# Weight remainders and branch sums made by accumulating transfers in a two-layer mixer trunk

## The chip, the core and the metric

The kernel runs on one core of a Trainium2 chip. The metric is the device time in microseconds of one execution of the whole program. The engines are TensorE (PE, matrix products), VectorE (DVE), ScalarE (ACT), GpSimd (POOL) and SyncE (SP, which only issues transfers). Each has its own instruction stream and runs it in order; transfers run on 16 shared engines of their own.

## The reference

Two layers over 512 latent tokens and 256 context tokens of width 1024, in float32. Cut to what matters here:

```python
h = rms(x) * (1 + scale) + shift             # scale, shift, gate from a small conditioning product
cols = h @ w_in                              # one projection, split for four mixers and their gates z
o_a = attention(q_a, k_a, v_a)               # rotary q and k, latent queries see all keys
o_d = windowed_attention(q_d, k_d, v_d, sink)
o_b = fourier_mix(b) ; o_c = spatial_gate(u, v)
y = stack([o * silu(z) for o, z in ...]) @ w_br          # per branch, to width 1024
g = sigmoid(h @ w_merge + b_merge)                       # per branch and channel
x = x + gate * (sum_over_branches(g * y) @ w_out)
```

In the second layer the context tokens are read but not updated.

## The kernel before

**Float32 products in three passes.** TensorE works on float32r, a rounded float32. To keep float32 accuracy every weight and every activation is held as two tiles: `hi`, the rounded value, and `lo`, the remainder (value minus `hi`). A product is then `hi*hi + hi*lo + lo*hi`, three matmuls into the same PSUM bank: L185, L186 (both with the weight's `wh`) and L188 (with the weight's `wl`).

**Weights come in pieces.** A list `plan` has 320 pieces in the order in which the program uses them: 256 of 128x512 elements (256 KB) and 64 of 128x256 (128 KB, the branch projections `w_br`). `wload` (L154) issues the load of a piece on SP into a raw tile `wr` (L159); `wround` (L162) casts it on ACT into `wh` (L169) and subtracts on POOL, or on DVE for one piece in three, into `wl` (L171). `wnext` (L174) is called when the program comes to a piece: it asks for loads up to five pieces on and for splits up to two on, so that when piece i is used, piece i+1 is being split. There are three buffers each of `wr`, `wh`, `wl`. A raw buffer is free for the next load when the subtraction has read it.

**Stages.** The start squares and norms x, computes the conditioning (`ada_tile`, weights `aw`) and, in the same loop over eight k-tiles, the first projection from pieces of its own (`wst`, tiles `ws`, split on ACT and POOL at L393 and L394). Each layer then projects (`proj`, `vproj`: `vproj("v")`, `uproj`, `qblock`, `zblock`, `bproj`), prepares rotary q and k (`Rope.finish`, with tables `cos` and `sin` loaded once into the constant tile `krope` at L405), rearranges them by transfers (`stack_k` L526, `stack_q` L513), and does attention with the projections and the merges of branches C and A as filler between its matmuls. Then come the merges of D and B (`merge`) at full matmul rate, and the output projection (`outp`). `merge` makes for each of eight channel tiles j a gate product (two pieces) and a branch product (one half piece), applies tanh on ACT (L669) and the product on DVE (L671) into a tile `g`, and adds it into `M[j]` at L674: on POOL for A and D, on DVE for the last branch B. Beside the merges and the output projection of layer 0 runs `ada_rest`, the conditioning of the second layer (64 loads `wadat` on SP, 128 reductions on DVE at L274).

**Between the layers** `outp` does its context-and-first-latent columns `c_a` and the rest `c_b` separately, and the second layer's first projection (`kv`, sixteen pieces `wkv`, first pass over 512 columns, second over 256) starts while the norms of the new x are applied (`Norm.apply`, L353 to L356).

**What sets the order.** Generators interleave the parts in program order, by estimated costs (`drive`, `paced`, `mix`); each engine's stream is then laid out from that order by the tile framework, which may move an instruction past others that it does not depend on.

Of the kernel before, what the change touches and what calls it, by code (L numbers as in the profile page):

```python
# [12 lines left out]
F32 = dt.float32  # L13
F32R = dt.float32r
BF16 = dt.bfloat16
AF = mybir.ActivationFunctionType
ALU = mybir.AluOpType
AX = mybir.AxisListType

P = 128  # L20
D = 1024
KT = 8
NL = 512
# [6 lines left out]
LOADS, W_RAW, W_HI, W_LO = 5, 3, 3, 3  # L30
# [17 lines left out]
def hybrid_trunk(tc, xt, cv, crow, win, wst, wkv, wm, wo, wada, wadat, sm, bsp, wsp, wfn, kc, krope, kmask,  # L48
                 kdft, dfl, dfc, out):
    nc = tc.nc  # L50
# [6 lines left out]
    with ExitStack() as es:  # L57
# [15 lines left out]
        def tl(tag, name, dtype=F32):  # L73
            return pools[tag].tile([P, NT], dtype, name=name, tag=tag)
# [77 lines left out]
        loaded, ready = [], []  # L152
# [9 lines left out]
        def wround(upto):  # L162

            while len(ready) < min(upto, len(plan)):
                i = len(ready)
                n, raw = plan[i][1], loaded[i]
                hi = pw.tile([P, 512], F32R, name=f"wh{i}", tag="whi", bufs=W_HI)
                lo = pw.tile([P, 512], F32R, name=f"wl{i}", tag="wlo", bufs=W_LO)
                A.copy(hi[:, :n], raw[:, :n])  # L169
                on_v = i % 3 == 0 if both[0] <= i < both[1] else i % 3 == 2 and i >= 24  # L170
                (V if on_v else G).tensor_sub(lo[:, :n], raw[:, :n], hi[:, :n].bitcast(F32))  # L171
                ready.append((hi, lo))

        def wnext():  # L174

            i = cnt[0]
            cnt[0] += 1
            wload(i + LOADS)
            wround(i + 2)
            return ready[i]  # L180
# [191 lines left out]
        rt_ = pc.tile([P, 2 * NL], F32, name="krope")  # L372
        cos, sin = rt_[:, :NL], rt_[:, NL:]
# [10 lines left out]
        for kk in range(KT):  # L384
# [9 lines left out]
            G.tensor_sub(wl[:, :512], wraws[kk][:, :512], wh[:, :512].bitcast(F32))  # L394
            if kk == 0:
                lat4 = [bank(f"st{b}", "mm" if b < 3 else "o") for b in range(4)]
                ctx4 = pps.tile([P, 1024], F32, name="stc", tag="s")
# [7 lines left out]
        nc.sync.dma_start(rt_, krope)  # L405
# [6 lines left out]
        for l in range(DEPTH):  # L412
# [9 lines left out]


# [31 lines left out]
            class Rope:  # L455
# [16 lines left out]
                def finish(self):  # L472
# [9 lines left out]
                    yield  # L482
                    r = tl("sc", f"r{name}")
# [162 lines left out]
            def merge(r, first=False, final=False, ctag="mm"):  # L646
                yb = YB[r]
                mlp = mq = None
                for j in range(KT):
# [23 lines left out]
                    if not first:  # L673
                        (V if final else G).tensor_add(M[j][:, WC], M[j][:, WC], g[:, WC])  # L674
# [228 lines left out]
            def stacks_a():  # L903

                yk = yield from rk.finish()
# [10 lines left out]
            def stacks_d():  # L916
                yq = yield from RQ[1].finish()
                yield from stack_q(Q[1], *yq, f"1{l}")
# [275 lines left out]
```

## Time and profile before

| | us |
|---|---|
| median of 3 runs | 1218.69 |
| lowest, highest | 1217.77, 1220.76 |
| the profiled execution, its own time | 1220.09 |
| its span, first to last instruction | 1218.2 |
| PE busy in the span | 1183.5 |
| DVE busy | 658.7 |
| ACT busy | 470.7 |
| POOL busy | 392.2 |

Busy time is the union of an engine's instructions; matmuls overlap, so their durations are longer than the distance from one start to the next. The profile page also gives the share of time in which the 16 transfer engines were busy, the queues' bytes, the waits of each engine by what ended them, and the chain of work that ended last.

### The profile page before, as it was taken

To read this page: it belongs to the slowest core of one execution; us is meant where nothing else is said; L and a number is where in the kernel's file an instruction comes from. 1 tells how busy PE (TensorE), PEld (TensorE's weight loads), DVE (VectorE), ACT (ScalarE), POOL (GpSimd) and SP (SyncE) were. 2 spreads that over 40 slices of the span, in tenths; PEclk is the share of its full clock that TensorE was granted. 3 is DMA by queue.
4 is the path that set the end of the run, shared out by engine and by line. 5 is a ranking of instruction groups with operands and counts; after the bars stand their busy time and mean duration, and the time that the engine had idled before them with its cause. 6 is when DMAs were issued, how large, how long until landed. Compare 5 with 4: busy or idle time off the path is not lost.

```text
span 1218.2 us, 18950 instructions
## 1 busy us (share of the span) xinstructions
PE 1183.5 (97%) x7164; PEld 1004.2 (82%) x7164; DVE 658.7 (54%) x1325; ACT 470.7 (39%) x933; POOL 392.2 (32%) x292
## 2 busy tenths in 40 slices
PE   5999999999999999999999998989999999999998
PEld 3798888888888888888888887877788888888887
DVE  5673446443455442588988667646645554232331
ACT  5334634333333332322333255445444444333431
POOL 1322333212212234454222234442222233454332
PEclk8999999999999999999999999999999999999999
DMA  7717213211111113345555653373322212333353
GB/s 282 256 31 172 79 37 83 73 36 61 53 44 49 44 56 83 93 153 160 180 165 193 183 163 110 117 194 75 99 62 69 71 56 77 101 87 100 95 166 124
DMA packets 73499, 131.99 MB, mean 108 GB/s; under 512 B 8769, under 2 KB 19137, under 8 KB 73409
## 3 DMA queue, kind: packets, MB, share of 16 engines
q1 hardware_dynamic: 66640, 120.30, 33.8%
q10 hardware_dynamic: 6768, 10.50, 2.8%
q8 instruction: 56, 0.92, 0.3%
q14 instruction: 35, 0.28, 0.1%
HBM read 115.03 MB, written 4.19 MB: 98 GB/s over the span
## 4 chain that ended last, share of the span: by engine, by line
PE 86%; DVE 5%; DMA 4%; issue 2%; ACT 2%; POOL 1%; SPq 1%; ACTq 0%; POOLq 0%
PE gl L185 10%; PE gl L186 10%; PE gl L188 10%; PE o L631 4%; PE gc L185 3%; PE tp L598 3%; PE gc L188 3%; PE gc L186 3%; PE ow L185 3%; PE ow L186 3%; PE ow L188 3%; PE yl L185 2%; PE yl L186 2%; PE yl L188 2%; PE p L185 2%; PE p L188 2%
## 5 line engine op out<-in xcount | busy, mean ns | idle before, releaser
L171 POOL TENSOR_TENSOR wl<-wr,wh 128x512 fp32r<-128x512 f32 (+1 forms) x222 | 287.5, 1297 | 703.7 <-ACT wh L169 665.4
L169 ACT CAST wh<-wr 128x512 fp32r<-128x512 f32 (+1 forms) x320 | 184.5, 577 | 354.3 <-PE gl L186 92.4
L185 PE MATMUL gl<-hh,wh 128*128 128x512 f32 x512 | 204.2, 399 | 0.0
L186 PE MATMUL gl<-hl,wh 128*128 128x512 f32 x512 | 200.2, 391 | 0.0
L188 PE MATMUL gl<-hh,wl 128*128 128x512 f32 x512 | 199.9, 391 | 0.0
L574 DVE TENSOR_REDUCE mx<-s 128x1 f32<-128x768 f32 (+3 forms) x80 | 61.6, 770 | 131.5 <-PE s L568 67.4
L171 DVE TENSOR_TENSOR wl<-wr,wh 128x512 fp32r<-128x512 f32 (+1 forms) x98 | 68.9, 703 | 116.8 <-ACT wh L169 116.5
L188 PEld LDWEIGHTS gl<-hh,wl 128*128 128x128 f32 x512 | 96.1, 188 | 21.1
L185 PEld LDWEIGHTS gl<-hh,wh 128*128 128x128 f32 x512 | 96.5, 188 | 16.6 <-issue 0.2
L186 PEld LDWEIGHTS gl<-hl,wh 128*128 128x128 f32 x512 | 96.5, 189 | 16.2
L274 DVE CUSTOM_DVE_ANT_0 aj<-at,cb 128x512 f32<-128x512 f32 x128 | 107.1, 876 | 1.5 <-DMA at<-in_wadat_dram 1.5
L582 ACT ACTIVATE p<-s,ng 128x768 f32<-128x768 f32 (+3 forms) x80 | 60.1, 751 | 97.1 <-DVE ng L579 55.5
L185 PE MATMUL gc<-hh,wh 128*128 128x256 f32 x256 | 73.5, 287 | 0.0
L188 PE MATMUL gc<-hh,wl 128*128 128x256 f32 x256 | 72.5, 283 | 0.0
L186 PE MATMUL gc<-hl,wh 128*128 128x256 f32 x256 | 72.3, 283 | 0.0
L185 PE MATMUL p<-hh,wh 128*128 128x512 f32 (+1 forms) x192 | 71.1, 370 | 0.2 <-DVE z L539 0.2
L185 PE MATMUL ow<-MH,wh 128*128 128x512 f32 (+1 forms) x200 | 69.5, 348 | 1.3 <-DVE nq1a L343 0.9
L188 PE MATMUL ow<-MH,wl 128*128 128x512 f32 (+1 forms) x200 | 69.4, 347 | 0.9 <-DVE wl L171 0.9
L186 PE MATMUL ow<-ML,wh 128*128 128x512 f32 (+1 forms) x200 | 69.4, 347 | 0.0
L188 PE MATMUL p<-hh,wl 128*128 128x512 f32 (+1 forms) x192 | 68.4, 356 | 0.0
L186 PE MATMUL p<-hl,wh 128*128 128x512 f32 (+1 forms) x192 | 68.1, 355 | 0.0
L669 ACT ACTIVATE g<-gl,bmh 128x512 f32<-128x512 f32 x64 | 43.8, 685 | 62.2 <-DVE macc L274 37.0
(466 smaller groups left out, 2583.6 us busy)
## 6 DMA issues: line engine op xcount, KB each, us to landing
wr<-in_wm_dram SPq DMA_DIRECT2D x128, 256.0 KB, 2.7
wr<-in_win_dram SPq DMA_DIRECT2D x72, 256.0 KB, 2.9
at<-in_wadat_dram SPq DMA_DIRECT2D x64, 256.0 KB, 2.8
wr<-in_wo_dram SPq DMA_DIRECT2D x40, 256.0 KB, 3.0
aw<-in_wada_dram SPq DMA_DIRECT2D x16, 512.0 KB, 5.8
wr<-in_wm_dram SPq DMA_DIRECT2D x64, 128.0 KB, 2.2
ks<-yk SPq DMA_DIRECT2D x32, 192.0 KB, 4.2
wr<-in_wkv_dram SPq DMA_DIRECT2D x16, 256.0 KB, 2.7
```

Of the source, the lines that this page charges most:

```text
L169: A.copy(hi[:, :n], raw[:, :n])
L171: (V if on_v else G).tensor_sub(lo[:, :n], raw[:, :n], hi[:, :n].bitcast(F32))
L185: T.matmul(d, wh, xh[:, c0:c1], start=first and op, stop=False)
L186: T.matmul(d, wh, xl[:, c0:c1], start=False, stop=False)
L188: T.matmul(d, wl, xh[:, c0:c1], start=False, stop=last and cl)
L274: V.tensor_tensor_reduce(out=junk[:, :512], in0=w[:, :512], in1=cb[2 * v + half][:, :512], scale=0.5, scalar=0.0, op0=ALU.mult, op1=ALU.ad ...
L574: V.reduce_max(out=mx, in_=sv, axis=AX.X)
L582: A.activation(p[:, :nk], sv, AF.Exp, bias=ng, scale=0.125, accum_out=sm_)
L598: T.transpose(tp[:, (i - g0) * P:(i - g0 + 1) * P], p[:, i * P:(i + 1) * P], ident)
L631: T.matmul(dst[64 * hx:64 * hx + 64, :], vt[kt_ // 3][:, kt_ % 3, c0:c0 + 64], pts[hx][:, j * P:(j + 1) * P], start=(j == 0), stop=(j == l ...
L669: A.activation(g[:, q0:q1], gp, AF.Tanh, scale=0.5, bias=bmh[:, r * 8 + j:r * 8 + j + 1])
```

## The change

- `wround` no longer subtracts. ACT writes `lo` as minus the raw piece, rounded as `hi` is (so `lo = -hi`), then `hi`, and POOL issues a transfer that reads the piece from DRAM again and adds it into `lo` (`accum_op=ALU.add`). All 320 pieces go this way; the raw buffer is free when ACT has read it twice.
- The buffers become 2 of `wr`, 5 each of `wh` and `wl`, and `wnext` splits up to five pieces on (piece i+4 when piece i is taken) and loads up to seven on.
- In the start's loop, at its third k-tile, the first seven loads and five splits of `plan` are asked for.
- In `merge`, the sums into `M[j]` of branches A and D become transfers from `g` to `M[j]` with the same addition, issued by POOL. Branch B stays on DVE.
- The rotary tables leave the constant tile (4 KB per partition): `tables` loads cos and sin, 256 KB each, on ACT's queue into two tiles of the pool `z`, once for the group of `stacks_a` and once for that of `stacks_d` in each layer.

```diff
-LOADS, W_RAW, W_HI, W_LO = 5, 3, 3, 3
+W_RAW, W_HI, W_LO, AHEAD = 2, 5, 5, 5
...
-                n, raw = plan[i][1], loaded[i]
+                (src, n), raw = plan[i], loaded[i]
...
+                A.activation(lo[:, :n], raw[:, :n], AF.Copy, scale=-1.0)
                 A.copy(hi[:, :n], raw[:, :n])
-                on_v = i % 3 == 0 if both[0] <= i < both[1] else i % 3 == 2 and i >= 24
-                (V if on_v else G).tensor_sub(lo[:, :n], raw[:, :n], hi[:, :n].bitcast(F32))
+                G.dma_start(lo[:, :n], src, accum_op=ALU.add)
...
-            wload(i + LOADS)
-            wround(i + 2)
+            wload(i + AHEAD + W_RAW)
+            wround(i + AHEAD)
...
+            if kk == 2:
+                wload(AHEAD + W_RAW)
+                wround(AHEAD)
...
-        nc.sync.dma_start(rt_, krope)
...
+            def tables(name):
+                if not TAB:
+                    for i in range(2):
+                        t = tl("z", f"rt{i}{name}")
+                        nc.scalar.dma_start(t[:, :NL], krope[:, i * NL:(i + 1) * NL])
+                        TAB.append(t[:, :NL])
+                return TAB
...
                     if not first:
-                        (V if final else G).tensor_add(M[j][:, WC], M[j][:, WC], g[:, WC])
+                        if final:
+                            V.tensor_add(M[j][:, WC], M[j][:, WC], g[:, WC])
+                        else:
+                            G.dma_start(M[j][:, WC], g[:, WC], accum_op=ALU.add)
```

Three places in the engines' streams. In the names, the number behind a tile's name counts pieces (`wl187` is the remainder of piece 187), k-tiles (`aw4_0`, `ws4`) or channel tiles.

**SP in the start's loop, before:** the loads of conditioning weights `aw` and first-projection pieces `ws`.

```order
L228 DMA aw4_0_408<-in_wada_dram 128x1024
L228 DMA aw4_4_414<-in_wada_dram 128x1024
L381 DMA ws4_457<-in_wst_dram 128x512
L381 DMA ws5_516<-in_wst_dram 128x512
L381 DMA ws6_575<-in_wst_dram 128x512
L228 DMA aw5_0_467<-in_wada_dram 128x1024
L228 DMA aw5_4_473<-in_wada_dram 128x1024
L381 DMA ws7_634<-in_wst_dram 128x512
L405 DMA krope_177<-in_krope_dram 128x1024
```

**SP in the start's loop, now:** the same loads with the first plan pieces `wr` between them.

```order
L159 DMA wr0_373<-in_win_dram 128x512
L159 DMA wr1_375<-in_win_dram 128x512
L379 DMA ws3_436<-in_wst_dram 128x512
L228 DMA aw4_0_446<-in_wada_dram 128x1024
L159 DMA wr2_377<-in_win_dram 128x512
L228 DMA aw4_4_452<-in_wada_dram 128x1024
L159 DMA wr3_379<-in_win_dram 128x512
L379 DMA ws4_495<-in_wst_dram 128x512
L159 DMA wr4_381<-in_win_dram 128x512
L228 DMA aw5_0_505<-in_wada_dram 128x1024
L159 DMA wr5_383<-in_win_dram 128x512
```

The plan's loads, which stood behind `aw6`, now stand between the loads of `aw4` and `aw5`, and `ws5` comes after them.

**ACT between the layers, before** (`sq1b`, `hh1` and `x2d`, `xr` belong to the norms and the residual of the output projection):

```order
L963 DMA xr06512_7522<-in_xt_dram 128x256
L355 ACTIVATE hh1_1_7402<-hx1a1_7561,mod1_119 128x256 x2
L169 CAST wh156_7595<-wr156_7524 128x512
L169 CAST wh157_7639<-wr157_7542 128x512
L169 CAST wh158_7670<-wr158_7575 128x512
L319 ACTIVATE sq1b6_7568<-xn6_6861 128x256
L1001 DMA x2d_127<-xn6_6861 128x512
L963 DMA xr07512_7573<-in_xt_dram 128x256
```

**ACT between the layers, now:**

```order
L977 DMA xr06512_7700<-in_xt_dram 128x256
L169 ACTIVATE wl157_7724<-wr157_7668 128x512
L170 CAST wh157_7723<-wr157_7668 128x512
L355 ACTIVATE hh1_1_7576<-hx1a1_7741,mod1_119 128x256 x2
L169 ACTIVATE wl158_7758<-wr158_7702 128x512
L170 CAST wh158_7757<-wr158_7702 128x512
L319 ACTIVATE sq1b6_7748<-xn6_7019 128x256
L1015 DMA x2d_127<-xn6_7019 128x512
L977 DMA xr07512_7753<-in_xt_dram 128x256
```

Each piece has two ACT instructions now, in the same places of the stream; the matmuls that they are for lie further on.

**POOL at the first layer-1 projections, before** (`st0q01` is rotary work, `u1` the spatial gate):

```order
L171 TENSOR_TENSOR wl187_8465<-wr187_8352,wh187_8464 128x512
L495 TENSOR_TENSOR st0q01_8061<-st1q01_8062,krope_177 128x512
L727 TENSOR_TENSOR u1_8164<-u1_8164,z301_8458 128x512
L171 TENSOR_TENSOR wl189_8540<-wr189_8436,wh189_8539 128x512
L171 TENSOR_TENSOR wl190_8573<-wr190_8462,wh190_8572 128x512
L727 TENSOR_TENSOR u1_8164<-u1_8164,z311_8498 128x512
```

**POOL at the same place, now:**

```order
L171 DMA wl189_8654<-in_win_dram 128x512
L504 TENSOR_TENSOR st0q01_8259<-st1q01_8260,rt1k1_8278 128x512
L171 DMA wl190_8681<-in_win_dram 128x512
L739 TENSOR_TENSOR u1_8370<-u1_8370,z301_8674 128x512
L171 DMA wl191_8700<-in_win_dram 128x512
L739 TENSOR_TENSOR u1_8370<-u1_8370,z311_8716 128x512
```

The rotary and gate multiplications stay on POOL; the subtractions between them are transfers now.

## Rows read from the trace of the kernel before

**Rows 1.** The page's head: span, and busy time, share and instructions of engines.

```profile
span 1218.2 us, 18950 instructions
...
PE 1183.5 (97%) x7164; PEld 1004.2 (82%) x7164; DVE 658.7 (54%) x1325; ACT 470.7 (39%) x933; POOL 392.2 (32%) x292
```

**Rows 2.** Waits of PE: total us, times, longest us.

```profile
PE p_q L185 <- DVE z L539: 3.1, 1, 3.1
PE ka L188 <- POOL wl L171: 2.8, 1, 2.8
PE p_cu L185 <- ACT vt L695: 2.5, 1, 2.5
PE n1b L341 <- DVE nq1b L320: 2.0, 1, 2.0
...
PE s L554 <- DMA qs<-yq: 1.0, 2, 0.5
PE ow L188 <- DVE wl L171: 0.9, 1, 0.9
```

**Rows 3.** Busy time by stretch of the span; the head names the columns.

```profile
core 0: us, PE busy (x) PEld busy (x) DVE busy (x) ACT busy (x) POOL busy (x), PEclk, DMA share, GB/s
30.00:60.00 30.00, 29.71 (x220) 22.31 (x222) 19.38 (x36) 12.12 (x23) 10.88 (x8) 1.00 0.76 252
90.00:130.00 40.00, 35.70 (x245) 32.61 (x244) 16.86 (x23) 16.96 (x31) 12.51 (x9) 1.00 0.72 167
553.00:637.00 84.00, 84.00 (x483) 74.05 (x482) 75.74 (x171) 25.70 (x45) 28.56 (x19) 1.00 0.56 167
711.00:775.00 64.00, 56.07 (x364) 49.77 (x363) 43.62 (x81) 34.39 (x71) 28.13 (x17) 0.97 0.45 138
810.00:860.00 50.00, 44.66 (x258) 35.38 (x257) 39.61 (x56) 22.74 (x41) 19.13 (x14) 0.97 0.34 93
1135.00:1180.00 45.00, 45.00 (x200) 37.24 (x200) 19.29 (x26) 18.57 (x32) 12.98 (x13) 1.00 0.43 127
```

**Rows 4.** Timeline of POOL and DVE: start us, us, what; [idle before].

```profile
86.53 1.75 POOL L171 TENSOR_TENSOR wl<-wr,wh 128x512 fp32r<-128x512 f32 x1 [0.81 <-ACT wh L169]
...
747.24 8.17 POOL L171 TENSOR_TENSOR wl<-wr,wh 128x512 fp32r<-128x512 f32 x2 [5.47 <-ACT wh L169]
...
814.52 1.77 DVE L171 TENSOR_TENSOR wl<-wr,wh 128x512 fp32r<-128x512 f32 x1
...
815.71 3.94 POOL L171 TENSOR_TENSOR wl<-wr,wh 128x512 fp32r<-128x512 f32 x2
```

**Rows 5.** Line 497 of DVE: ns least/median/most, first to last start.

```profile
L497 DVE TENSOR_TENSOR stk<-stk,krope x2: 2301/2304/2308, 87.1 to 784.3; 128x1024 f32<-128x1024 f32 x2
L497 DVE TENSOR_TENSOR st1q<-st1q,krope x2: 1211/1757/2303, 95.6 to 816.2; 128x1024 f32<-128x1024 f32 x2
```

**Rows 6.** Timeline of PE in the output projection's second columns.

```profile
720.45 0.28 PE L188 MATMUL ow<-MH,wl 128*128 128x256 f32 x1
720.57 0.28 PE L185 MATMUL ow<-MH,wh 128*128 128x256 f32 x1
```

**Rows 7.** Groups by line: busy us, mean ns | idle before, releaser.

```profile
L169 ACT CAST wh<-wr 128x512 fp32r<-128x512 f32 (+1 forms) x320 | 184.5, 577 | 354.3 <-PE gl L186 92.4
...
L674 POOL TENSOR_TENSOR M<-M,g 128x768 f32<-128x768 f32 x16 | 32.3, 2017 | 23.7 <-DVE g L671 23.7
```

**Rows 8.** Transfers: queue totals, then issues with size and us to landing.

```profile
q1 hardware_dynamic: 66640, 120.30, 33.8%
...
wr<-in_wm_dram SPq DMA_DIRECT2D x128, 256.0 KB, 2.7
...
qs<-yq SPq DMA_DIRECT2D x8, 256.0 KB, 4.7
```

**Rows 9.** Stretches of four microseconds, columns as in rows 3.

```profile
10.00:14.00 4.00, 3.94 (x9) 1.77 (x8) 2.20 (x4) 3.54 (x5) 0.00 (x0) 1.00 1.04 405
...
112.00:116.00 4.00, 4.00 (x35) 4.00 (x35) 0.00 (x0) 0.62 (x1) 0.33 (x1) 1.00 0.93 219
```

More of the change, by code (lines that the diff above doesn't have):

```diff
@@ L151, in hybrid_trunk @@
                 plan += outw(l, WHOLE)
-        loaded, ready = [], []
+        loaded, ready, TAB = [], [], []
         def wload(upto):
@@ L371, in hybrid_trunk @@
         kb = pc.tile([P, 3 * P], BF16, name="kbf")
-        rt_ = pc.tile([P, 2 * NL], F32, name="krope")
-        cos, sin = rt_[:, :NL], rt_[:, NL:]
         identb, mprev, mnext = kb[:, :P], kb[:, P:2 * P], kb[:, 2 * P:]
@@ L482, in finish @@
                     yield
+                    cos, sin = tables(name)
                     r = tl("sc", f"r{name}")
@@ L903, in stacks_a @@
             def stacks_a():
+                TAB.clear()
                 yk = yield from rk.finish()
@@ L916, in stacks_d @@
             def stacks_d():
+                TAB.clear()
                 yq = yield from RQ[1].finish()
```

## Prediction, made before the changed kernel was run

> **What bounds the kernel now.** I read the page's head first: PE is busy 1183.5 of 1218.2 us, so all waits of PE together are worth 34.7 us, under 3% [rows 1]. Next I read the stretches of the span, to see where those 34.7 us lie: in the merges PE is busy without a gap (84.00 of 84, and 45.00 of 45), while it stands idle for 4.3 us in 90 to 130, for 7.9 in 711 to 775 and for 5.3 in 810 to 860 [rows 3]. The rest is mostly the first 30 us, which the change leaves alone. Then the waits of PE say what ended those gaps [rows 2]. Two are waits for a remainder itself: the second layer's first projection for a POOL subtraction (2.8 us) and the output projection for a DVE subtraction (0.9). Two more are waits for DVE or ACT work that was late: 3.1 us for the gate z, 2.5 for the copies of v. So no gain beyond some 1.5% is to be had, and what the change brings must come from these four waits; a loss has no such limit, because every piece now hangs on a transfer of a kind that this trace does not show.
>
> **The removed subtractions as a disturbance.** POOL and DVE slow each other when both read pairs of tiles. Two POOL subtractions that start at 747.24 take 8.17 us [rows 4], and the wait of 2.8 us for `wl` falls there. On the DVE side the same rotary multiplication takes 1.21 us at its best and 2.30 in the disturbed cases, at 87.1 and at 816.2 among others [rows 5]; POOL runs subtractions at just those times, 1.75 us from 86.53 and 3.94 from 815.71 [rows 4]. With the change POOL holds no subtraction there, only the rotary and gate products that it had before.
>
> **Gains, step by step.**
> 1. The waits of 2.8 and 0.9 us for a remainder go: 3.7. They go because a piece is split four ahead, not because the new way is quicker. Four pieces last 4 x 12 matmuls x 0.12 = 5.8 us in the fastest place, where a piece feeds twelve matmuls of 256 columns at 0.12 us from start to start [rows 6], and 4 x 12 x 45.00/200 = 10.8 us in the second layer's merges [rows 3].
> 2. The wait of 3.1 us for z: ahead of z in DVE's stream stand a subtraction of 1.77 us, which goes altogether [rows 4], and the multiplication that is 1.09 us too long [rows 5]. That is 2.9 us from these two, and I count the 3.1 as gone.
> 3. The wait of 2.5 us for the copies of v: ACT reaches them only behind the rotary work, whose multiplication at 87.1 is 1.1 us too long [rows 5] while POOL subtracts. POOL's own rotary product stays, and disturbs too. I take 1.5.
> The sum of the gains is 8.3 us. The wait of 2.0 us for the norm `n1b` I leave standing.
>
> **Costs.** ACT gets a second pass over each of 320 pieces. The nearest row is the cast, 184.5 us for all [rows 7], so ACT goes from 470.7 to some 655 us, still little more than half of the span. Where it matters is 711 to 775: 24 pieces x 0.577 (the cast's mean [rows 7]) = 14 us more, on 34.39 of 64 [rows 3]. That is 48 of the 56 us that PE needs there, and in the places with 1.44 us per piece the two instructions take 1.15. Ahead of them in ACT's stream stand norm work and residual transfers that wait for DVE. Between 0 (the lead of 5.8 us covers it) and 7.9 (all of today's idle time comes back) I take 2.0, near the lower end, since the total still fits.
>
> The accumulating transfer appears nowhere in the trace. Its floor is a plain load: the SP queue moved 120.30 MB in 33.8% of 1218.2 us, 3.42 us per MB, so 0.90 us of all engines for a piece of 0.262 MB [rows 8]. It must read its destination as well as its source, so I take twice that, 1.8 us. The far end is the slowest row of that size, a rearranging transfer that needs 4.7 us to land against 2.7 for a weight load [rows 8]; read as if the engines were held all that time, 4.7 us. For the engines' load in 1135 to 1180: 200/12 = 16.7 pieces x 1.8 = 30 of 45 us, a share of 0.67 on top of 0.43 [rows 3], 1.10 together. The share overstates: with deep queues 405 GB/s ran at 1.04 [rows 9], 389 per full share, against 127/0.43 = 295 here, so 1.10 counts as 1.10 x 295/389 = 0.83 of what the engines can do. The same sum gives 0.76 in 553 to 637 (483/24 = 20 pieces, 0.43 on top of 0.56) and, in 711 to 775 compressed to 56 us, (0.45 x 64 + 24 x 1.8)/56 x 0.76 = 0.97. So only the last is tight; that is in the 2.0 above. At 0.90 us a piece nothing is tight.
>
> The Trainium skill bears on this term alone: "Collectives: The Full Stack", section "The bandwidth ceiling: the fold count and why AG ≠ RS ≠ AR", says that an addition inside the transfer engines needs two source reads and so runs at half the rate of a copy. By that page of the Trainium skill a piece holds the engines for 1.8 us (an estimate), which gives the 0.97; by the plain-load row alone it is 0.9, which gives 0.68 and takes at most 2.0 us off the sum. No row here shows which.
>
> Two places are busy already. In 90 to 130 the rearranging transfers fill the engines (0.93 in 112 to 116 [rows 9]) and PE's first score waits for the last of them, 1.0 us in two waits, at most 0.5 in one [rows 2]. Four accumulations fall there, 0 to 4 x 1.8 = 7.2 us; PE's stream has a few matmuls more ahead of that score, and more raw loads are done before: I take 1.0. In the start SP now issues seven piece loads among the conditioning loads, and POOL five accumulations, while the engines are at 0.76 [rows 3]: between 0 and 5 x 1.8 = 9, and I take 0.5, because SP's stalls on raw buffers there last only until ACT's casts.
>
> At nothing I count four edits. The loads of rotary tables on ACT's queue come well before use, behind transfers already in the stream; if that cover fails, a landing of 2.7 us is exposed once per group. The 32 sums into `M` (2.0 us each on POOL [rows 7]) are needed only a whole branch later, and their engine time is 16 x 1.5 x 1.8 + 16 x 1.8 = 72 us over both layers, spread; without that cover `g` would come free late and hold up ACT's tanh, and with it a PSUM bank. POOL issues instead of computing; what queues behind an issue that waits for DVE's `g` is the next remainder, which has four pieces' time.
>
> Net: -8.3 + 2.0 + 1.0 + 0.5 = -4.8 us. The profiled execution took 1220.09 us by its own time, which comes to 1215.3; it lies 1.4 above the median of 1218.69, which comes to 1213.9.
>
> **Rivals.**
> *A, about the same.* The four waits go, but between the layers ACT becomes the late engine, in order behind waits for DVE, and the full 7.9 us comes back there; with the 1.5 us of the two busy places the net is 8.3 - 7.9 - 1.5 = -1 us: 1217.6. For it: ACT's 48 of 56 us. Against: four pieces of lead.
>
> *B, slower, one mechanism: the transfer engines run full.* A piece's accumulation holds them too long, the lead is used up, and PE waits for `wl` in every full-rate stage. It decides first between the layers, where the share reaches 1 at c = (56/0.76 - 28.8)/24 = 1.9 us a piece, then in the second layer's merges and output projection, at (1/0.76 - 0.43) x 45/16.7 = 2.4 us. At c = 2.8: between the layers (28.8 + 67) x 0.76 = 73 us, 9 more than now; from 1040 to the end 178 us with 178/2.7 = 66 pieces, (0.43 x 178 + 185) x 0.76 = 199, 21 more; less the 4.6 us of gains 2 and 3, 25 more: 1244. At c = 2.4 the same sum gives 3 us less than now, so B is slower from about 2.5 on; at 4.7 it costs over 100. For it: the range of 0.9 to 4.7 that the trace leaves, and that its first threshold of 1.9 is close to my 1.8. Against: landing times of 2.7 us and a reserve of a third in the share.
>
> *C, not what it says.* If the transfers of POOL were slow to issue, splits four ahead would still come late; the signs are those of B with idle transfer engines. I count it with B.
>
> **How the numbers follow.** The forecast has a chance of 0.42, A 0.26, B with C 0.32. Measurements of this kernel can tell about 0.3%, 3.7 us, from no change; the forecast lies just beyond. The forecast's own range is 1206 (8.3 and the 2.0 of `n1b` gone, the costs nothing, and some 2 us more from the granted clock, which is 0.97 in two stretches after PE's idle time [rows 3]) to 1215; A covers 1215 to 1222. Two in ten are left out by cutting B at 1240, some way under its price at c = 2.8. So 1206 to 1240; faster 0.42, the same 0.26, slower 0.32.
>
> **What will show it.** Right: in 711 to 775 and 810 to 860 PE's idle time falls from 13.2 us to under 7; no row of waits from L188 for `wl`; the multiplication of line 497 near 1.21 us wherever POOL only issues; ACT near 655 us busy. A shows as idle time in 711 to 775 ended by ACT or by `wl` with short transfers. B shows as waits of L188 ended by transfers into `wl`, in the merges from 1040 on, where there are none now, with the transfer share above 0.9. I would be wrong altogether if the start or the first attention scores slip by more than 5 us.

## The result, and the profile after

The changed kernel takes 1311.28 us, median of four runs (1308.24 to 1316.51), against 1218.71 for the kernel before (1217.77 to 1220.76): a ratio of 1.076, 95% interval 1.072 to 1.081. It is 93 us slower; 1214 was forecast.

The first fence has the page's head, the transfer queues (packets, MB, share of 16 engines' span) and three rows of landing times of the changed kernel. They answer to [rows 1] and [rows 8].

```profile
span 1312.4 us, 19542 instructions
PE 1217.5 (93%) x7164; PEld 1019.6 (78%) x7164; DVE 541.1 (41%) x1227; ACT 619.2 (47%) x1253; POOL 355.7 (27%) x390
...
q0 software_dynamic: 50688, 86.01, 40.5%
q1 hardware_dynamic: 66496, 119.77, 31.2%
...
wr<-in_wm_dram SPq DMA_DIRECT2D x128, 256.0 KB, 4.1
wl<-in_wm_dram POOLq DMA_DIRECT2D x128, 256.0 KB, 4.6
...
wl<-in_wo_dram POOLq DMA_DIRECT2D x40, 256.0 KB, 6.2
```

PE now stands idle for 94.9 us in place of 34.7, and its busy time has grown by 34 us although it does the same matmuls. Part of that is the granted clock, which was 0.994 over the run before and is 0.974 here (0.89 to 0.95 in four of the five stretches shown next): by that ratio 1183.5 us become 1208, an estimate. What makes the other 10 us or so stays open. The adding queue `q0`, which carries the remainders and the sums into `M`, moves 86.01 MB in 40.5% of 1312.4 us: 6.18 us per MB, 1.62 us of all engines for a 256 KB piece, against 3.42 per MB for plain loads, which is still the figure of q1 (31.2% for 119.77 MB). A weight load that landed after 2.7 us now needs 4.1.

The time is lost in three parts of about the same size. The output projection of layer 0 starts 29.8 us later than before (at 686.0, not 656.2), the second layer's last query-projection matmul of L185 another 30.6 us (at 897.3, not 836.9), and the span ends another 34 us later. So the stretches below don't hold quite the same work as those before (columns as in [rows 3]); they show the merges of layer 0, the part between the layers, and the second layer's merges. The merges of both layers had PE busy without a gap (84.00 of 84 and 45.00 of 45 in [rows 3]).

```profile
560.00:640.00 80.00, 71.39 (x383) 61.98 (x383) 47.52 (x136) 29.17 (x57) 21.70 (x25) 0.94 0.89 215
...
720.00:800.00 80.00, 68.61 (x365) 58.44 (x363) 34.98 (x79) 45.50 (x90) 21.95 (x26) 0.89 0.91 209
800.00:880.00 80.00, 62.66 (x350) 53.35 (x350) 24.60 (x30) 44.03 (x81) 25.19 (x28) 0.95 0.93 203
1100.00:1150.00 50.00, 42.73 (x200) 35.15 (x199) 9.27 (x25) 20.71 (x43) 22.20 (x25) 0.93 0.81 164
1150.00:1200.00 50.00, 44.59 (x186) 33.95 (x185) 4.13 (x6) 21.24 (x42) 20.17 (x24) 1.00 0.95 188
```

The waits of PE and of ACT (line waited for, us in total, times, longest), which answer to [rows 2]:

```profile
PE gc L185 <- DVE g L680: 11.9, 6, 3.1
PE ow L188 <- DMA wl<-in_wo_dram: 11.6, 9, 2.9
PE gl L188 <- DMA wl<-in_wm_dram: 10.7, 14, 1.6
...
PE kvb L188 <- DMA wl<-in_wkv_dram: 7.1, 6, 2.4
...
PE p_q L185 <- DVE z L548: 4.4, 1, 4.4
```

```profile
ACT wh L170 <- DMA wr<-in_wm_dram: 76.5, 37, 9.2
...
ACT wl L169 <- DMA wr<-in_win_dram: 51.3, 21, 8.2
...
ACT wh L170 <- DMA wr<-in_wo_dram: 44.3, 19, 4.8
...
ACT g L678 <- DMA M<-g: 34.5, 5, 7.8
```

PE waits for remainders as never before, now for their transfers. But behind that ACT waits for raw pieces (172 us in three rows), which the forecast put at nothing outside the start. Fourteen microseconds of the timeline of the second layer's merges show how (start, duration, engine, line, operation, count; in brackets the idle time before it and what ended it; PE left out):

```profile
1107.96 8.01 SPq L159 DMA_DIRECT2D wr<-in_wm_dram  x4
1108.22 0.86 POOL L171 DMA_DIRECT2D wl<-in_wm_dram  x1 [0.64 <-ACT wl L169]
1111.46 0.62 ACT L170 CAST wh<-wr 128x512 fp32r<-128x512 f32 x1 [3.53 <-DMA wr<-in_wm_dram]
1111.99 0.63 ACT L169 ACTIVATE wl<-wr 128x512 fp32r<-128x512 f32 x1
1112.52 0.67 ACT L678 ACTIVATE g<-gl,bmh 128x512 f32<-128x512 f32 x1
1112.91 0.86 POOL L171 DMA_DIRECT2D wl<-in_wm_dram  x1 [3.83 <-ACT wl L169]
...
1115.10 1.22 POOL L686 DMA_DIRECT2D M<-g  x1
...
1121.28 0.62 ACT L170 CAST wh<-wr 128x512 fp32r<-128x512 f32 x1 [5.66 <-DMA wr<-in_wm_dram]
```

SP can ask for a piece only when ACT has read one of the two raw buffers; the load then lands late; until then ACT stands still, with the tanh of a finished merge tile (L678 at 1112.52) behind the casts in its order; then POOL issues the addition, which is itself a landing away. In this part the five buffers of `wh` and `wl` don't fill up (from 1100 to 1200 ACT waits 43.5 us for raw pieces and 2.2 for a buffer that a `gl` matmul of L186 still reads), so the lead of four pieces isn't there. In the merges of layer 0 it is there: ACT waits 67.6 us for buffers that `gc` matmuls of L186 still read. All of ACT's 34.5 us for `M<-g` lie in layer 0 as well, and some 12 of the 29.8 us lost there are the sums': with them on POOL, in the first experiment, the output projection starts at 673.8.

### The profile page after: what moved, and what is told of

The parts are those of the page before. It is cut to its first block, busy times and chain, and to the rows that moved or that the text cites. A ratio compares the mean times of both kernels' runs of the same rounds, so it can differ in the third digit from the quotient of the medians.

```text
span 1312.4 us, 19542 instructions
## 1 busy us (share of the span) xinstructions
PE 1217.5 (93%) x7164; PEld 1019.6 (78%) x7164; DVE 541.1 (41%) x1227; ACT 619.2 (47%) x1253; POOL 355.7 (27%) x390
## 3 DMA queue, kind: packets, MB, share of 16 engines
q0 software_dynamic: 50688, 86.01, 40.5%
q1 hardware_dynamic: 66496, 119.77, 31.2%
## 4 chain that ended last, share of the span: by engine, by line
PE 52%; DMA 16%; issue 15%; POOL 7%; DVE 5%; ACT 3%; SPq 3%; ACTq 0%; POOLq 0%; DVEq 0%
DMA wr<-in_wm_dram 7%; POOL wl L171 6%; PE gl L185 5%; PE gl L186 5%; PE gl L188 5%; PE o L640 3%; PE tp L607 3%; DMA wr<-in_win_dram 3%; PE gc L185 2%; PE p L185 2%; PE p L186 2%; PE p L188 2%; PE gc L186 2%; PE gc L188 2%; PE s L563 1%
## 5 line engine op out<-in xcount | busy, mean ns | idle before, releaser
L171 POOL DMA_DIRECT2D wl<-in_wm_dram x192 | 170.8, 895 | 489.4 <-ACT wl L169 407.1
L169 ACT ACTIVATE wl<-wr 128x512 fp32r<-128x512 f32 (+1 forms) x320 | 187.0, 584 | 101.4 <-DMA wr<-in_win_dram 51.3
L188 PE MATMUL gl<-hh,wl 128*128 128x512 f32 x512 | 204.1, 399 | 11.0 <-DMA wl<-in_wm_dram 10.7
L185 PE MATMUL gl<-hh,wh 128*128 128x512 f32 x512 | 205.9, 402 | 0.0
L186 PE MATMUL gl<-hl,wh 128*128 128x512 f32 x512 | 202.1, 395 | 0.0
L188 PEld LDWEIGHTS gl<-hh,wl 128*128 128x128 f32 x512 | 97.0, 189 | 40.6 <-DMA wl<-in_wm_dram 19.9
L171 POOL DMA_DIRECT2D wl<-in_win_dram x72 | 62.7, 873 | 227.6 <-ACT wl L169 212.3
L186 PEld LDWEIGHTS gl<-hl,wh 128*128 128x128 f32 x512 | 97.6, 191 | 16.7
L185 PEld LDWEIGHTS gl<-hh,wh 128*128 128x128 f32 x512 | 97.4, 190 | 16.3 <-issue 0.2
L274 DVE CUSTOM_DVE_ANT_0 aj<-at,cb 128x512 f32<-128x512 f32 x128 | 83.3, 687 | 45.0 <-DMA at<-in_wadat_dram 43.0
L680 DVE SCALAR_TENSOR_TENSOR g<-g,yl 128x512 f32<-128x512 f32 x48 | 33.0, 687 | 161.6 <-ACT g L678 126.1
L185 PE MATMUL gc<-hh,wh 128*128 128x256 f32 x256 | 75.4, 294 | 11.9 <-DVE g L680 11.9
L188 PE MATMUL ow<-MH,wl 128*128 128x512 f32 (+1 forms) x200 | 72.9, 365 | 11.6 <-DMA wl<-in_wo_dram 11.6
L678 ACT ACTIVATE g<-gl,bmh 128x512 f32<-128x512 f32 x64 | 43.6, 681 | 77.8 <-PE gl L188 38.1
L185 PE MATMUL ow<-MH,wh 128*128 128x512 f32 (+1 forms) x200 | 71.9, 360 | 2.3 <-ACT MH L692 1.4
L188 PE MATMUL gc<-hh,wl 128*128 128x256 f32 x256 | 73.5, 287 | 0.0
L186 PE MATMUL gc<-hl,wh 128*128 128x256 f32 x256 | 73.4, 287 | 0.0
L186 PE MATMUL ow<-ML,wh 128*128 128x512 f32 (+1 forms) x200 | 72.0, 360 | 0.2 <-DVE ML L693 0.2
L185 PE MATMUL p<-hh,wh 128*128 128x512 f32 (+1 forms) x192 | 70.9, 370 | 0.0
```

Of the source, the lines that this page charges most:

```text
L169: A.activation(lo[:, :n], raw[:, :n], AF.Copy, scale=-1.0)
L171: G.dma_start(lo[:, :n], src, accum_op=ALU.add)
L185: T.matmul(d, wh, xh[:, c0:c1], start=first and op, stop=False)
L186: T.matmul(d, wh, xl[:, c0:c1], start=False, stop=False)
L188: T.matmul(d, wl, xh[:, c0:c1], start=False, stop=last and cl)
L274: V.tensor_tensor_reduce(out=junk[:, :512], in0=w[:, :512], in1=cb[2 * v + half][:, :512], scale=0.5, scalar=0.0, op0=ALU.mult, op1=ALU.ad ...
```

## The experiments

Three theories were put up first. T1: the transfer engines are full. T2: two raw buffers are too few. T3: the sums by transfer hold `g`, and with it ACT and a PSUM bank.

**Undoing one part, or sizes.** Four kernels from the changed one. The sums back on POOL:

```diff
-G.dma_start(M[j][:, WC], g[:, WC], accum_op=ALU.add)
+G.tensor_add(M[j][:, WC], M[j][:, WC], g[:, WC])
```

> The changed kernel (1311 us) with one part undone: the 32 sums into M of branches A and D are additions on POOL again. Theory T1, the 16 transfer engines are full where the matmuls run at full rate: the sums are 10.5 MB of 88.6 MB added, so about an eighth of the 93 us comes back, 1295 to 1305. Theory T2, two raw buffers and a landing of 4 to 5 us set the pace of the pieces: no more than 5 us, 1306 to 1312. Theory T3, the transfers out of g hold its three buffers, so that ACT's tanh (34.5 us of waits in 5) and with it a PSUM bank come late: 30 us or more come back, below 1280.

Measured 1288.03 (1282.94 to 1298.02): 23 us back, between T1's and T3's numbers. ACT's wait for `M<-g` is gone, and PE's wait for `g` falls from 11.9 to 4.6 us.

The remainders back to subtractions:

```diff
-A.activation(lo[:, :n], raw[:, :n], AF.Copy, scale=-1.0)
 A.copy(hi[:, :n], raw[:, :n])
-G.dma_start(lo[:, :n], src, accum_op=ALU.add)
+(V if on_v else G).tensor_sub(lo[:, :n], raw[:, :n], hi[:, :n].bitcast(F32))
```

> The changed kernel with the other part undone: remainders are subtractions on POOL and DVE again (one ACT pass fewer), all else as changed: two raw buffers, five of wh and wl, splits four ahead, tables by transfer, sums by transfer. T1: seven eighths of the loss come back, 1220 to 1240. T2: the raw buffers are held even longer (until the subtraction), so it stays above 1290. T3: the sums still hold g, 1260 to 1300.

Measured 1228.08 (1226.34 to 1230.76): 83 us back, as T1 said. T2 alone and T3 alone fall: buffers and sums are as changed here, and cost little.

Four buffers of each kind:

```diff
-W_RAW, W_HI, W_LO, AHEAD = 2, 5, 5, 5
+W_RAW, W_HI, W_LO, AHEAD = 4, 4, 4, 4
```

> The changed kernel with four buffers each of wr, wh and wl and splits three ahead instead of 2, 5, 5 and four ahead; the same bytes and instructions. T1: full engines are not helped by a deeper queue of loads, 1300 to 1316. T2: with four raw buffers the loads overlap, ACT's 172 us of waits for wr go, and 50 us or more come back, below 1260. T3: about as changed, 1300 to 1315.

Measured 1262.85 (1257.50 to 1263.85): 48 us back with the same bytes and instructions, just short of what T2 asked for (50 or more, below 1260). So T1 alone falls as well.

Half of every addition:

```diff
-G.dma_start(lo[:, :n], src, accum_op=ALU.add)
+G.dma_start(lo[:64, :n], src[:64], accum_op=ALU.add)
```

> The changed kernel in which each accumulating transfer into a weight's lo covers 64 of the 128 partitions (the other half of lo stays minus hi: that part of the products is left out); number of instructions and waits as changed, 36 MB of added bytes fewer, in rows of the same 2 KB. T1: about 225 us of the transfer engines' time go, and with them half the loss or more, 1245 to 1275. T2: the loads land little earlier and ACT's stream is the same, 1285 to 1311. T3: 1290 to 1311.

Measured 1243.67 (1243.21 to 1245.35): 68 us back without a buffer changed, as T1 said, and a little more.

**All eight combinations.** The parts act together, so the remaining cells were run, by combining the three edits above; four buffers, subtractions and sums on POOL; four buffers and sums on POOL; four buffers and subtractions; subtractions and sums on POOL.

> The kernel before (1218 us) with what is left of the change when nothing is added by transfers: remainders by subtraction, sums on POOL and DVE, but four buffers each of wr, wh, wl, splits three ahead, the first requests in the start's loop, tables loaded by transfer when needed. T1 (the transfer engines are full because of the adds) and T2 (two raw buffers): no adds and four raw buffers, so 1210 to 1220; the waits of the matmuls for remainders (3.7 us in before) should fall below 1. If the forecast's gain for splits ahead is real, it shows here as 2 to 5 us below before.

> The changed kernel with both helpful edits of the first four runs: four buffers each of wr, wh, wl (which gave 48 us) and the sums into M on POOL (23 us); only the remainders are added by transfers. If the two act on different waits, 1311 - 48 - 23 = 1240; if on the same waits (ACT held up, by late raw pieces or by g), 1248 to 1262. T1 alone (engines full from the remainders' adds): 1245 or more, with the engines' share near .9 still in the slow stretches. T2 alone: 1220 to 1235.

> One of two cells that are missing of eight (remainders added or subtracted, sums by transfer or on POOL, four or two raw buffers): subtracted, sums by transfer, four buffers each. The sums cost 21 to 23 us where remainders are added (1311 to 1288, 1263 to 1242). If that is the transfers' own hold on g, it is the same here: 1219 + 21 = 1240. If it is their share of full transfer engines, there is room here (share near 0.55 in the merges) and they cost under 5: 1219 to 1224.

> The other cell: subtracted, sums on POOL, two raw buffers with five of wh and wl and splits four ahead. Two raw buffers cost 46 to 48 us where remainders are added. If two raw buffers are too few by themselves, 1219 + 47 = 1266. If they are too few only because loads that share the engines with the adds land after 4 us in place of 2.7, they cost little here: 1219 to 1228.

| remainders | sums into `M` | 2 wr, 5 wh, 5 wl | 4, 4, 4 |
|---|---|---|---|
| added by transfer | by transfer | 1311.28 (the change) | 1262.85 |
| added by transfer | on POOL | 1288.03 | 1241.83 |
| subtracted | by transfer | 1228.08 | 1217.82 |
| subtracted | on POOL | 1225.41 | 1219.24 |

The two columns differ in the number of buffers and in the lead, four pieces against three. Read by columns and rows: with subtractions the buffer sizes are worth 6.2 and 10.3 us and the sums between 2.7 lost and 1.4 gained; with additions the buffers are worth 46 and 48 and the sums 21 and 23. The additions are the condition, and by themselves, with four buffers and the sums on POOL, they cost 22.6 us (1241.83 - 1219.24). The two expectations that asked which of two readings holds (1240 or 1219 to 1224 for the sums, 1266 or 1219 to 1228 for the raw buffers) both came out on the side of the loaded engines, at 1217.82 and 1225.41. With additions the gains of sums and buffers add up, as was expected if they act on different waits (1240, measured 1241.83). The landing times fit: `M<-g` of 384 KB took 6.4 us in the changed kernel and has ACT waiting 34.5 us; with subtractions and four buffers it takes 5.1, ACT waits 11.2 us for it, in four waits, and PE none. ACT's wait for raw pieces, on the other hand, is no measure of the loss by itself: with subtractions, sums on POOL and two raw buffers it is still 121 us (48.3 + 46.7 + 18.2 + 8.1), and that kernel takes 1225.41.

The stretch from 560 to 640, in the merges of layer 0, shows where the sums cost: PE had 71.39 of 80 us in the changed kernel. The rows are those of four buffers with the sums by transfer, of two raw buffers with the sums on POOL, and of four buffers with the sums on POOL:

```profile
560.00:640.00 80.00, 71.33 (x383) 61.25 (x382) 45.90 (x129) 29.04 (x57) 19.49 (x23) 0.96 0.91 220
```

```profile
560.00:640.00 80.00, 76.47 (x436) 66.22 (x435) 60.55 (x150) 32.13 (x61) 24.39 (x25) 1.00 0.91 220
```

```profile
560.00:640.00 80.00, 80.00 (x460) 70.50 (x459) 64.31 (x157) 35.34 (x66) 25.62 (x27) 1.00 0.94 233
```

Here the buffers alone give nothing back, the sums alone 5 us, and both together all of it.

What four buffers do to the second layer's merges is plain in the run with additions, sums on POOL and 4, 4, 4 (same columns):

```profile
720.00:800.00 80.00, 67.29 (x410) 57.45 (x409) 39.29 (x81) 54.31 (x109) 27.54 (x31) 1.00 0.96 221
800.00:880.00 80.00, 72.75 (x420) 60.58 (x419) 39.01 (x60) 46.90 (x83) 25.25 (x26) 0.96 0.84 191
1100.00:1150.00 50.00, 50.00 (x222) 41.34 (x222) 6.41 (x10) 27.64 (x54) 26.66 (x29) 1.00 0.99 194
1150.00:1200.00 50.00, 49.93 (x220) 40.95 (x219) 15.04 (x22) 30.47 (x57) 18.21 (x22) 1.00 0.98 209
```

In the merges PE runs without a gap although the transfer engines are at 0.98 and 0.99, more than the changed kernel's 0.81 and 0.95. Full engines are no loss there as long as enough is on its way; with two raw buffers they weren't even full. Between the layers PE has 140.0 of 160 us, against 151.7 in the run at 1219.24 (subtractions, sums on POOL, four buffers).

**Raw buffers or lead?** The changed kernel with four raw buffers, but three of `wh` and `wl` and splits two ahead, and the same with a fourth buffer for `g`:

```diff
-W_RAW, W_HI, W_LO, AHEAD = 2, 5, 5, 5
+W_RAW, W_HI, W_LO, AHEAD = 4, 3, 3, 3
...
-"sc": pool("sc", 3)
+"sc": pool("sc", 4)
```

> The changed kernel with four raw buffers, three of wh and wl and splits two ahead: remainders and sums by transfer. Against 2, 5, 5 (1311) and 4, 4, 4 (1263). If the raw buffers make the difference, 1258 to 1275; if the lead of the splits counts as much, 1280 or more. It is also the base of the next run.

> The same with four buffers in the pool of g instead of three. If the sums cost 21 us because a transfer out of g, landing after some 6 us, holds the buffer that the next tanh wants (35 us of ACT's waits in 5), 12 us or more come back against the run with three. If it is the bytes of the sums on full engines, less than 5.

Measured 1338.87 (1336.93 to 1343.27) and 1330.41 (1325.07 to 1338.88). My reading that raw buffers make the difference by themselves falls: with four of them but splits only two ahead it is 76 us slower than 4, 4, 4 and 28 slower than the change. The waits of the first of the two say why, those of PE and then one of ACT that the second doesn't have:

```profile
PE gl L188 <- DMA wl<-in_wm_dram: 51.4, 46, 5.2
PE ow L188 <- DMA wl<-in_wo_dram: 20.9, 20, 2.7
```

```profile
ACT g L678 <- DMA M<-g: 30.3, 6, 6.6
```

Now ACT hardly waits for raw pieces (7.6 us in its list of waits), but in the merges PE waits 46 times for an addition that hasn't landed yet. The same sizes and lead with subtractions and the sums on POOL take 1219.36 (the second kernel under "What the gain was worth"), so the short ring is dear only beside transfers that add. Both rings must hold a landing: the raw ring that of the load, the ring of `wl` that of the addition. The fourth buffer of `g` takes away all of ACT's 30.3 us, but gives only 8.5 us, between the two expectations (12 or more, under 5). The hold on `g` is real; how much of the sums' 21 to 23 us it makes, and how much their bytes, stays open, since in this pair PE is held by `wl` first.

**The last 23 us.** Is it ACT's second pass, the engines' capacity, or the path of a piece? From the run at 1219.24, ACT also writes minus the raw piece, which the subtraction then overwrites:

```diff
+A.activation(lo[:, :n], raw[:, :n], AF.Copy, scale=-1.0)
 A.copy(hi[:, :n], raw[:, :n])
```

> The run with subtraction, sums on POOL and four buffers (1219) in which ACT also writes minus the raw piece into lo before hi, as in the changed kernel; the subtraction overwrites it. No adding transfers. It prices ACT's second pass, 187 us of ACT's time, alone. If ACT's stream is what the last 23 us wait for (rival A of the forecast), 1227 to 1242; if there is room for it, 1217 to 1222.

Measured 1217.31 (1216.15 to 1219.06). ACT is busy 619.3 us, as in the changed kernel, and nothing is lost. From the run at 1241.83, half of each addition, every other piece, or only the pieces away from the start and from the stretch between the layers:

The first has the edit of `lo[:64, :n]` above. In the second a piece for which `add` is false gets `hi` and the subtraction as before; in the third `add` is `4 <= i < 84 or i >= 176`:

```diff
+add = i % 2 == 1
+if add:
+    A.activation(lo[:, :n], raw[:, :n], AF.Copy, scale=-1.0)
 A.copy(hi[:, :n], raw[:, :n])
+if add:
+    G.dma_start(lo[:, :n], src, accum_op=ALU.add)
+else:
+    (V if on_v else G).tensor_sub(lo[:, :n], raw[:, :n], hi[:, :n].bitcast(F32))
```

> The run with four buffers each and the sums on POOL (1242, of which the same with subtraction is 1219) with the accumulations over 64 of 128 partitions: the other half of lo stays minus hi, so that part of the products is left out. Same instructions and buffers. If the last 23 us are the capacity of the transfer engines between the layers and at the start (share 0.96 to 1.00 there), most of them go: 1219 to 1227. If they are the path of a piece (two casts, an issue on POOL, a landing), a third at most goes: 1233 to 1242.

> Four buffers each, sums on POOL, splits three ahead; every other piece is added by transfer and its neighbour subtracted on POOL or DVE. Half the added bytes of the run at 1242, as in the run with half of the partitions (1216), but a complete computation. If capacity is the whole of the last 23 us, 1213 to 1219; if a piece's path through the add counts too, half of the 23 stays: 1227 to 1232. Subtractions on DVE and POOL disturb each other again, so the wait for the copies of v may come back.

> The same, but added are the 80 pieces of layer 0's projections and of its merges C and A, and the 144 of the second layer from its attention's projections on; the start, the merges D and B of layer 0 and everything between the layers subtract. 224 of 320 pieces are added, none where the engines' share reached 0.96 with PE idle. If that stretch alone made the last 23 us, 1213 to 1219, though the share stays at 0.98 in the second layer's merges; if full engines cost wherever they are full, 1225 to 1240.

Half partitions: 1215.87 (1214.13 to 1223.08; interval of the ratio 0.9965 to 1.0004), so all of the 23 us and a little more come back, which I took for capacity. Every other piece: 1235.23 (1229.74 to 1239.88), with as many bytes gone, and only 7 us back, less than either expectation had (1213 to 1219 or 1227 to 1232). So bytes are not the whole of it. The landing row of `wl` in the merges, first of the full run, then with half partitions, then with every other piece:

```profile
wl<-in_wm_dram POOLq DMA_DIRECT2D x128, 256.0 KB, 4.7
```

```profile
wl<-in_wm_dram POOLq DMA_DIRECT2D x128, 128.0 KB, 3.3
```

```profile
wl<-in_wm_dram POOLq DMA_DIRECT2D x64, 256.0 KB, 4.3
```

And the stretches between the layers with every other piece (columns as in [rows 3]):

```profile
720.00:800.00 80.00, 68.82 (x403) 61.41 (x402) 47.01 (x84) 46.21 (x91) 34.80 (x27) 0.91 0.69 168
800.00:880.00 80.00, 73.29 (x425) 61.16 (x424) 44.14 (x66) 42.35 (x73) 25.29 (x23) 0.96 0.68 159
```

Half partitions shorten each landing to 3.3 us; every other piece leaves it at 4.3, and PE is idle for 17.9 of 160 us with the engines at 0.69. That speaks for the landing of a single piece. It isn't shown: additions and subtractions also share POOL's order in that run.

By place: 1227.83 (1225.28 to 1231.73), 224 of 320 pieces added and 8.6 us above the run with none. That is in the range expected if full engines cost wherever they are full, but not for that reason: the second layer's merges have a share of 0.97 to 1.00 and lose under a microsecond (PE 99.23 of 100). One part of the loss is where additions meet transfers that PE waits for: in 90 to 130 PE has 31.97 of 40 us (36.37 with subtractions), by this wait, which was 1.1:

```profile
PE s L569 <- DMA qs<-yq: 7.6, 1, 7.6
```

The other is in 760 to 840, where it has 71.7 of 80 against 75.6, as the second layer's additions begin: there PE waits 2.5 us for remainders that haven't landed, and 4.9 in place of 3.7 for z.

**The load alone, badly measured.** Two kernels with subtractions, three buffers each, and one more transfer of every piece into a spare tile:

```diff
+G.dma_start(scr[i % 3][:, :n], src, accum_op=ALU.add)
```

and the same as a plain copy, without `accum_op`.

> Subtraction and sums as in the kernel before, three buffers each, tables by transfer; beside it, for every piece, POOL issues one more accumulating transfer of the piece from DRAM into one of three spare tiles that nothing reads. It carries the load of the change on the transfer engines without putting the adds in any piece's path. T1 (contention alone): loads land late as in the changed kernel (4 us or more for 256 KB), 1250 to 1300. T4, the path (load, two casts, add, each in turn, in a short ring) and not the load on the engines: 1218 to 1230.

> As the run with the extra accumulating transfers, but the extra transfers are plain copies of the same pieces into the spare tiles, issued by POOL too. At 0.90 us of the engines each in place of 1.62, T1: a third to a half of the other's loss (1225 to 1255). T4: 1218 to 1228, no difference between the two.

Measured 1540.90 and 1358.90. They don't answer the question: since nothing ties these transfers to a place, they were ordered far ahead (in the first kernel all are issued by 651 of 1537 us), and there POOL waits for the spare tiles (243 us in two rows) with the subtractions behind it. What they do give is the price of an addition at a share of 0.93, the mean of the first 600 us: 75.52 MB in 31.6% of 1537.4 us, 6.43 us per MB, against 17.3% of 1353.5, 3.10, as plain copies.

**What the gain was worth.** Two kernels with subtractions and earlier splits, without the requests in the start's loop, the first from the run at 1219.24, the second from the kernel before:

```diff
-if kk == 2:
-    wload(AHEAD + W_RAW)
-    wround(AHEAD)
...
-LOADS, W_RAW, W_HI, W_LO = 5, 3, 3, 3
+LOADS, W_RAW, W_HI, W_LO = 7, 4, 3, 3
...
-wround(i + 2)
+wround(i + 3)
```

> The run with subtraction, sums on POOL, four buffers and splits three ahead (1219), without the requests in the start's loop. In 30 to 60 us its PE had 26.5 of 30 us against 29.7 in before, with a wait of 2.7 for the conditioning weights; after that it was ahead. If the early requests cost that, 1214 to 1217; if the start catches up by itself, 1218 to 1220.

> The kernel before with one raw buffer more, loads seven on and splits one piece further ahead (requested three on, still three buffers of wh and wl): no transfer adds, the tables stay in their constant tile, no requests in the start. It takes from the change what the first gain of the forecast rests on. If splitting ahead removes the waits for remainders (3.7 us), 1214 to 1217; if the time comes back elsewhere, 1218 to 1220.

Measured 1218.54 (ratio 0.9991, interval 0.9983 to 0.9999) and 1219.36 (1.0000). Neither reaches 0.3%. In the second, with three buffers of `wl`, the wait for a remainder stays (3.8 us); in the first it is down to 0.3, but PE has 26.56 us in 30 to 60 where it had 29.71 [rows 3], without any early request, so those were not to blame. The quickest complete kernels, ACT's idle second pass (0.9987) and the sums by transfer with subtractions (0.9988), are 0.1% under before. Their intervals (0.9977 to 0.9996 and 0.9980 to 0.9997) just leave out 1, but no version comes near the 0.3% that the prediction named as what can be told from no change.

## Why the prediction was wrong

- **Gain 1, the step that failed.** "A piece is split four ahead" was read as 5.8 to 10.8 us of lead, and that lead was to cover the additions too. A lead exists only if the splits are made in time, and nothing was put down for the raw buffers going from 3 to 2, outside the start. A raw buffer is held for a load of 4.1 us and two casts, 1.2 together, so two of them give a piece every 2.65 us at best (an estimate from these rows). The merges use one in 2.7, which leaves nothing for a late request or a busy ACT, and then come the issue and an addition of 4.6. The sizes cost 46 to 48 us under additions, 6 to 10 under subtractions. The two old waits didn't go but changed hands: `ka` waits 2.0 us for a transfer where it waited 2.8 for POOL, `ow` 11.6 where it waited 0.9 for DVE, and all waits for transfers into `wl` are 36 us. Even without additions the gain isn't there: with four buffers the waits for remainders fall to 0.3 us, and the kernel takes 1219.24.
- **The additions themselves** were mis-sized: 3.5 us was put down for them and ACT's second pass (2.0, 1.0 and 0.5), and with four buffers and the sums on POOL they cost 22.6. Against the same kernel with subtractions, 15.5 us lie, in the profiled executions, between the start of layer 0's output projection and the second layer's last query projection, 4.3 before and 2.0 behind.
- **Gain 2** failed as well. DVE's work ahead of z shrank as forecast, but PE still waits 4.4 us: z's chain begins later, behind a square on ACT (L207), which stands in ACT's order among casts that wait for raw pieces. From line 208 to z DVE takes 8.1 us where it took 11.4, so DVE's subtraction was not what PE's wait hung on here. The rows are the start of the chain, the late multiplication and z in the changed kernel; the subtraction of [rows 4] is gone from before the multiplication:

```profile
870.70 0.69 DVE L208 SCALAR_TENSOR_TENSOR st0q<-st0q 128x512 f32<-128x512 f32 x1 [9.36 <-ACT st0q L207]
...
875.38 1.23 DVE L506 TENSOR_TENSOR st1q<-st1q,rt0k 128x1024 f32<-128x1024 f32 x1
...
878.80 0.67 DVE L548 SCALAR_TENSOR_TENSOR z<-z,p 128x512 f32<-128x512 f32 x1
```

- **Gain 3** held: the multiplication of line 497 (L506 now) takes 1.21 to 1.23 us in all six places, against up to 2.31 [rows 5], and the wait for the copies of v fell from 2.5 to 0.4. It was small beside the rest.
- **ACT's second pass**, in the 2.0, costs nothing where it was tried alone, with subtractions and four buffers; beside additions it wasn't tried alone. ACT is busy 619 us, not 655. Rival A is out by its time, and by its cause: from 720 to 880 ACT waits 59 us for raw pieces and 7 for DVE.
- **The addition's price** was right: 1.8 us forecast, 1.62 measured, 1.8 to 2.1 times a plain transfer. The far end of 4.7 is out. The Trainium skill's page "Collectives: The Full Stack", section "The bandwidth ceiling: the fold count and why AG ≠ RS ≠ AR", gives two source reads and half a copy's rate for the adding step of a ring of cores. The traces agree with it for the additions of this kernel, at those 1.8 to 2.1.
- **The reserve** was wrong. Shares were scaled by 0.76 because 405 GB/s had been seen at 1.04 [rows 9]. Between the layers, with four buffers, the engines stood at 0.96 with 221 GB/s and PE idle. The unscaled sum, (28.8 + 24 x 1.62) = 67.7 us for a stretch that was to shrink to 56, points that way. The share alone doesn't prove it, since with every other piece added PE was idle there at 0.69. In the second layer's merges the loads do fit, at 0.99, but only with four buffers of each kind.
- **The sums at nothing**: the text named what happens without their cover, and that happened: ACT's tanh waits 34.5 us for `M<-g`, and PE 11.9 for `g` (4.6 with the sums on POOL). They cost 21 to 23 us, under additions only.
- **Rival B** had the sign, and one of its marks: L188 waiting for `wl` from 1040 on (16.7 us). Its mechanism, full engines, isn't what held the merges: the share was 0.81 and 0.95 there, and at 0.99 with four buffers PE loses nothing. It counted the engines' time and not the landings, so its threshold of 2.5 us a piece was wrong: the loss came at 1.62, and at 1311 it is far beyond B's 1244 and the range's end of 1240. B's sum has nothing for the first layer either, where a third was lost. **C** is out: an issue takes 0.9 us (170.8 us for 192), and POOL is busy 27% and mostly waits for ACT.

The sum of the parts, taken away from the changed kernel one after the other: 23 (sums) + 46 (buffers) + 23 (additions) = 92 of the 93 us. The shares hang on this order, since the parts act together: the additions taken away first are worth 83. What stays open is how the last 23 divide between the landing of single pieces and the engines' full share, and the sums' 21 between hold and bytes.

## What to carry to other kernels

A split "n ahead" is worth n pieces only if every ring on the way holds the landing that it covers: count for each buffer what fills it, what frees it, and the landing time under the new load, not the old one. An engine's share near 1 isn't a loss by itself; what loses is a short ring, or a transfer on the critical path that now lands later. When work moves to the transfer engines, price it where they already bound something, and look for transfers that hold a buffer which an in-order engine wants.

## What the hardware showed that I had not expected

The same plain load of 256 KB lands after 2.7 us beside subtractions and after 4.1 us beside additions, with the engines at 0.8 to 0.95 and not full. The share alone doesn't set it: with four buffers and the sums on POOL the load lands after 3.4 us, with the engines at 0.94 to 0.99 in the merges, and with every other piece added after 2.7 again.

Idle PE is paid for a second time afterwards: 60 us more idle time came with 34 us more busy time for the same matmuls. One place shows how. Ahead of the wait of 4.41 us for z, at 866, `p` matmuls of 512 columns start every 0.23 us. Behind it, from 880 to 885, `p_q` matmuls of the same size start every 0.43 us, at a granted clock of 0.50, the lower of its two levels (1.2 and 2.4 GHz); by 889 they are back at 0.23 and 1.00.
